# Layer 1's pooling mixer and cross-attention in one plan, its queries by seven products; readers of a PSUM bank due by the bank's next user

## The chip, the cores and the metric

The kernel runs on one core of a Trainium2 chip. Five engines work beside each other, each through its own instructions in order: PE (TensorE, matrix products), DVE (VectorE), ACT (ScalarE), POOL (GpSimd) and SP (here the queue that issues all the DMAs). They wait for each other by semaphores. The metric is the device time of one execution in microseconds. All data are float32; a product of two float32 matrices is made from three matmuls on a "high" and a "low" part of each operand (`mm3`: high·high, high·low, low·high), in a reduced format called fp32r.

## The reference, cut to what matters

```python
def reference(x, mem, ...):
    for i in range(2):
        if i == 0:                                   # layer 0
            x = x + axial_gqa_attention(rmsnorm(x, attn_norm[0]), ...)
        else:                                        # layer 1
            x = x + multiscale_pool_mixer(rmsnorm(x, pool_norm[0]), pool_w[0], pool_scale[0])
        x = x + memory_cross_attention(rmsnorm(x, xattn_norm[i]), rmsnorm(mem, mem_norm[i]),
                                       xattn_w_q[i], xattn_w_kv[i], xattn_w_o[i])
        x = x + conv_gated_ffn(rmsnorm(x, ffn_norm[i]), ...)
    return rmsnorm(x, final_norm)

def multiscale_pool_mixer(h, w_grp, scale):          # h is (1024, 1024)
    # per group of 256 channels: centred mean over 2/4/8/16 tokens, minus the token itself,
    # then a 256x256 matrix per group, and a scale per channel
    mixed = (s_hi - s_lo) / count - hg
    return einsum('bsgc,gcd->bsgd', mixed, w_grp) * scale

def memory_cross_attention(h, mem_n, w_q, w_kv, w_o):  # 4 heads of 256, 256 memory tokens
    q = h @ w_q * 256 ** -0.5                        # (1024, 1024) @ (1024, 1024)
    k, v = split(mem_n @ w_kv)
    return softmax(q @ k.T) @ v @ w_o
```

## The kernel before, in words

The 1024 tokens are eight row tiles `X[0]` to `X[7]` of 128 rows by 1024 columns, which stay in SBUF. There are 20 operand tiles `R` (each in two halves), and six scratch tiles `scr` of 128 x 1024. PSUM is two buffers `pA` of 1024 columns and four banks `pB` of 512.

Most of the program is made by a planner (class `Plan`). A function hands it operations, each with the engine, an assumed duration, what it reads and writes, which buffers it takes, and sometimes a due time `late`. The operations on PE stay in the order in which they were handed over. Those of the other engines are sorted by a due time, counted back from the PE operation that needs them, and the planner then writes every engine's instructions in that order. The attention of layer 0 and, before the change, the pooling mixer and cross-attention of layer 1 are written out by hand instead.

The large products of layer 0's cross-attention (its queries) and of both gated MLPs go by class `Seven`: Strassen's scheme with seven products instead of eight. Eight block sums of the right operand (`B11`, `B21`, `B22`, `T1` to `T4`) are made from the transposed row tiles, in pairs of an even and an odd tile, and block sums of the weights (`A11`, `A12`, `S1` to `S4`, `A22`) on DVE. A transposed row tile goes through `turn` (PE, eight transpositions), `take1` and `take2` (ACT and DVE).

The stage that the change touches lies between the last products of layer 0's MLP and the output matrix of layer 1's cross-attention. Before, it runs so:

- `pool_weights` fetches the mixer's weights and scales them, behind the plan of layer 0's MLP.
- `pool_mixer` goes through 16 steps. In each, the entries of `POOL_ORDER` are called in turn, each with a lag in steps. "rest" (`down`, L1747 on) makes two products of six matmuls for one row tile and adds them to `X` (DVE, L1757); "fetch" (L1800) copies a piece of 128 rows, shifted against the tiles so that each gives 112 rows of means, from `X` to a scratch tile by DMA; "scale" normalises it (square on ACT L651, 1/rms on POOL L643 and L645, scaling on ACT L1812); "mix" (L1819) multiplies it with a band matrix on PE; its result is split into high and low on ACT (L590) and DVE (L591); "out" makes the group matrices' products (24 matmuls of 256 columns) and adds them to `X` (DVE, L1836); "norm" (L656) and "turn" (L664) normalise and transpose a row tile for the queries; "go" makes the first queries.
- `cross_queries` makes the rest of the queries by plain products of 24 matmuls of 512 columns, 16 of them, and in between halves of the sums of layer 1's MLP weights (`down_sums`, L1418). `cross` then makes the memory's keys and values, scores, softmax (ACT L1352, POOL L1356) and values. `X` stays where it is during all this.

```python
POOL_ORDER = ((0, "rest"), (2, "stage"), (3, "split"), (5, "norm"), (1, "fetch"), (10, "go"), (6, "split2"),
              (4, "stage2"), (12, "go2"), (4, "out"), (1, "scale"), (2, "mix"), (5, "turn"))
```

Of the kernel before, what the change touches and what calls it, by code (L numbers as in the profile page):

```python
# [16 lines left out]
P = 128  # L17
# [13 lines left out]
XH = 4  # L31
# [7 lines left out]
POOL_ORDER = ((0, "rest"), (2, "stage"), (3, "split"), (5, "norm"), (1, "fetch"), (10, "go"), (6, "split2"),  # L39
              (4, "stage2"), (12, "go2"), (4, "out"), (1, "scale"), (2, "mix"), (5, "turn"))  # L40
# [43 lines left out]
class Slots:  # L84
# [43 lines left out]

    def put_half(self, *hs):
        self.clock += 1  # L130
        for h in hs:
            self.freed[h] = self.clock if self.now is None else self.until

    def v(self, i, a):
        return self.tiles[i].rearrange("p (a b) -> p a b", a=a)

# [4 lines left out]
class Plan:  # L141
# [18 lines left out]
    def add(self, kind, n, emit, reads=(), writes=(), take=(), uses=(), gives=None, late=None):  # L160


        engine, least, each, lag = self.KINDS[kind]
# [23 lines left out]

    def run(self):
        pools = self.pools
        for op in reversed(self.ops):  # L190
            for o in op["after"]:
                o["due"] = min(o["due"], op["due"] - o["lag"])
# [60 lines left out]
        self.slots.timed(False)  # L253


class Seven:
# [6 lines left out]
    def __init__(self, kn, w, columns, X, Xd, gain):  # L263
        self.kn, self.nc, self.R = kn, kn.nc, kn.R
        self.w, self.columns, self.X, self.Xd, self.gain = w, columns, X, Xd, gain
        self.H, self.raws, self.place, self.ops, self.bank, self.ps, self.r = {}, {}, {}, {}, {}, {}, {}

# [136 lines left out]
    def begin(self, gemm, add, free, between):  # L404

        late, split = self.late, self.split
# [26 lines left out]

    def plan_rest(self, plan):

        X = lambda t, h: (f"X{t}", h)
        nc, lo, hi = self.nc, self.LO, self.HI

        def keep(name, t, src, *keys, uses=()):
            parts = lambda: self.parts(name, t)  # L440
            shaped = lambda: src().rearrange("p (a b) -> p a b", a=4)
            plan.add("copy", 512, lambda: self.kn.high(list(parts())[0], shaped()), keys, [("H", name, t)], uses=uses)
            plan.add("add", 512, lambda: self.kn.low(*parts(), shaped()), [*keys, ("H", name, t)], [("H", name, t)], uses=uses)

        def sub(out, p, q, reads, writes, uses=(), late=None):
            plan.add("add", 512, lambda: self.sub(nc.vector, out(), p(), q()), reads, writes, uses=uses, late=late)

        t = NT - 1
        x, y = self.X[t - 1], self.X[t]
        ps = lambda g: lambda: self.ps[t][g]  # L450
        at = lambda ap, h: lambda: ap[:, h]
# [1494 lines left out]
```

## Time and profile before

| | |
|---|---|
| median of 3 runs | 2574.74 us (2573.03 to 2577.07) |
| the profiled execution | 2578.49 us, its span 2576.7 us |
| PE busy | 2516.0 us, 98% of the span |
| DVE, ACT, POOL busy | 1950.9, 1329.6, 380.6 us |
| the stage that the change touches | 1547.36 to 1832.76 us of the span |

In the views, a line such as L1757 is a line of the kernel before; `out<-in` are the tiles' names without their numbers; `PEld` is PE loading weights, which overlaps `PE`. A matmul's recorded end is modelled, so a busy PE can still be waiting a little. The rows of windows give busy time of each engine, with the number of instructions in brackets, then the granted clock of PE as a share of full speed (`PEclk`), the share of DMA time and GB/s. A row of the time line ends with the idle time of the engine before it and what ended it.

### The profile page before, as it was taken

How to read it: one execution, taken by the hardware profiler on the slowest of the kernel's cores; microseconds unless marked ns; L12 is line 12 of the kernel's file. 1: busy time of each engine (PE TensorE's matmuls, PEld its weight loads, DVE VectorE, ACT ScalarE, POOL GpSimd, SP SyncE). 2: the span in 40 equal slices, each digit the busy share in tenths (PEclk: the TensorE clock that was granted, in tenths of full speed). 3: DMA queues.
4: the chain of work that ended last, by engine and by line, in shares of the span. 5: the costliest groups of instructions: out<-in, count | busy, mean ns of one | idle time of the engine just before them, and what ended most of it. 6: DMA issues, size and time to landing. Idle time of an engine off the chain costs nothing. (4 is left out here: it accounts for less than half of the span.)

```text
span 2576.7 us, 36870 instructions
## 1 busy us (share of the span) xinstructions
PE 2516.0 (98%) x13529; PEld 2149.3 (83%) x13529; DVE 1950.9 (76%) x2857; ACT 1329.6 (52%) x2244; POOL 380.6 (15%) x523
## 2 busy tenths in 40 slices
PE   8999999999999999999999998999999999999998
PEld 7988888888898888888877887889788888887886
DVE  5778999974886389888878756654559988888775
ACT  4447888863555255555455425424436554555441
POOL 3664554530002000000000001102010000000001
PEclk9999999999999999999999999999999999999999
DMA  4200000042485134243358633581223333337751
GB/s 157 83 9 1 1 2 1 2 152 66 160 310 206 42 90 123 82 123 103 94 175 275 209 125 91 179 311 50 88 78 94 113 91 113 113 98 267 235 184 65
DMA packets 289801, 306.79 MB, mean 119 GB/s; under 512 B 12245, under 2 KB 230717, under 8 KB 289621
## 3 DMA queue, kind: packets, MB, share of 16 engines
q1 hardware_dynamic: 289621, 304.45, 36.5%
q8 instruction: 106, 1.74, 0.3%
q14 instruction: 74, 0.61, 0.1%
HBM read 223.04 MB, written 76.55 MB: 116 GB/s over the span
## 5 line engine op out<-in xcount | busy, mean ns | idle before, releaser
L670 PE MATMUL pB<-R,R 128*128 128x512 f32 (+1 forms) x2708 | 1013.5, 375 | 4.5 <-ACT R L590 1.9
L671 PE MATMUL pB<-R,R 128*128 128x512 f32 (+1 forms) x2708 | 1007.0, 372 | 1.8 <-DVE R L591 1.7
L672 PE MATMUL pB<-R,R 128*128 128x512 f32 (+1 forms) x2700 | 1003.3, 372 | 2.5 <-DVE R L585 2.5
L670 PEld LDWEIGHTS pB<-R,R 128*128 128x128 f32 x2708 | 510.2, 189 | 98.5 <-ACT R L590 3.0
L671 PEld LDWEIGHTS pB<-R,R 128*128 128x128 f32 x2708 | 510.4, 188 | 90.3 <-DVE R L591 3.5
L672 PEld LDWEIGHTS pB<-R,R 128*128 128x128 f32 x2700 | 508.4, 188 | 91.6 <-DVE R L585 3.3
L582 ACT ACTIVATE R<-scr 128x512 fp32r<-128x512 f32 (+2 forms) x283 | 205.8, 760 | 207.3 <-PE pB L671 58.0
L643 POOL TENSOR_SCALAR ms<-ss 128x1 f32<-128x1 f32 (+2 forms) x102 | 27.3, 267 | 1698.8 <-ACT scr L651 675.0
L585 DVE TENSOR_TENSOR R<-X,R 128x512 fp32r<-128x512 f32 x339 | 228.9, 686 | 65.1 <-ACT R L582 65.1
L582 ACT ACTIVATE R<-X 128x512 fp32r<-128x512 f32 x339 | 210.9, 630 | 100.5 <-PE pB L671 64.5
L585 DVE TENSOR_TENSOR R<-scr,R 128x512 fp32r<-128x512 f32 (+2 forms) x283 | 232.4, 851 | 13.9 <-ACT R L582 13.8
L394 ACT COPY scr<-pB 128x512 f32<-128x512 f32 x144 | 84.4, 587 | 187.9 <-PE pB L672 182.5
L664 PE MATMUL pB<-ident,scr 128*128 128x128 f32 x1232 | 163.8, 276 | 10.3 <-DVE scr L656 7.9
L664 PEld LDWEIGHTS pB<-ident,scr 128*128 128x128 f32 x1232 | 140.7, 143 | 35.6 <-POOL scr L729 14.9
L729 POOL TENSOR_SCALAR scr<-scr,inv 128x1024 f32<-128x1024 f32 x128 | 144.6, 1129 | 166.6 <-DVE inv L728 161.7
L670 PE MATMUL pA<-R,R 128*128 128x512 f32 (+1 forms) x460 | 161.6, 351 | 6.7 <-ACT R L582 2.3
L1673 DVE TENSOR_TENSOR X<-pB,X 128x512 f32<-128x512 f32 x144 | 99.3, 691 | 89.3 <-PE pB L672 86.8
L591 DVE TENSOR_TENSOR PT<-pB,PT 128x512 fp32r<-128x512 f32 x256 | 163.9, 681 | 3.0 <-ACT PT L590 2.0
L726 ACT ACTIVATE scr<-pA,nm 128x1024 f32<-128x1024 f32 x128 | 143.0, 1117 | 44.6 <-DVE nm L723 42.5
L672 PE MATMUL pA<-R,R 128*128 128x512 f32 (+1 forms) x460 | 160.8, 350 | 1.7 <-DVE R L591 0.8
L671 PE MATMUL pA<-R,R 128*128 128x512 f32 (+1 forms) x460 | 160.1, 348 | 0.5 <-DVE R L585 0.5
L723 DVE TENSOR_REDUCE nm<-pA 128x1 f32<-128x1024 f32 x128 | 156.1, 1219 | 0.9 <-PE pA L719 0.4
(157 smaller groups left out, 3596.7 us busy)
## 6 DMA issues: line engine op xcount, KB each, us to landing
X<-in_ffn_w_up SPq DMA_DIRECT2D x82, 512.0 KB
scr<-in_ffn_w_down SPq DMA_DIRECT2D x54, 512.0 KB
Gs<-X SPq DMA_DIRECT2D x100, 256.0 KB
scr<-Gs SPq DMA_DIRECT2D x56, 384.0 KB
scr<-Wt SPq DMA_DIRECT2D x40, 512.0 KB
scr<-in_xattn_w_kv SPq DMA_DIRECT2D x32, 512.0 KB
Wt<-scr SPq DMA_DIRECT2D x60, 256.0 KB
scr<-Gs SPq DMA_DIRECT2D x28, 512.0 KB
```

Of the source, the lines that this page charges most:

```text
L394: self.nc.scalar.copy(out, p)
L582: self.nc.scalar.activation(hi, src, AF.Copy)
L585: self.nc.vector.tensor_tensor(out=lo, in0=src, in1=hi.bitcast(F32), op=OP.subtract)
L591: nc.vector.tensor_tensor(out=lo, in0=src, in1=hi.bitcast(F32), op=OP.subtract)
L664: self.nc.tensor.transpose(p[:, k, :], src[:, b * P:(b + 1) * P], self.ident)
L670: mm(out, ah, bh, start=start, stop=False)
L671: mm(out, ah, bl, start=False, stop=False)
L672: mm(out, al, bh, start=False, stop=stop)
L723: nc.vector.tensor_reduce(nm, s, axis=AX.X, op=OP.max, negate=True)
L726: nc.scalar.activation(pr, s, AF.Exp, bias=nm, accum_out=rs)
L729: nc.gpsimd.tensor_scalar(pr, pr, ri, 1.0, op0=OP.mult, op1=OP.mult)
L1673: nc.vector.tensor_tensor(out=x, in0=banks[b], in1=x, op=OP.add)
```

## The change

`pool_mixer`, `cross_queries`, `cross` and `memory` of layer 1 go; the planned function that made layer 0's cross-attention (`cross_planned`, now `cross`) makes both layers'. For layer 1 it first hands the planner the mixer (`MIXER`: D for the last products of layer 0's MLP, M for mix, O for out, T for a row tile's transpositions and its block sums, in the order even tiles first), then the queries as seven products for each of four pairs of column blocks. A piece's scaling goes from ACT to POOL. `X` is saved to DRAM (`Xq1`) after the mixer, since its tiles are then used as buffers, and loaded again at the end. The mixer's weights are prepared inside the plan of layer 0's MLP, at the start of its third round. In all plans, `releases` gives those operations that read a PSUM bank a due time before the PE operation that takes the bank next; a set of operand tiles is taken when its first part is written, and the transposed probabilities may lie in single halves (`get_pair`).

```diff
-POOL_ORDER = (...)
+MIXER = ("D0", "D1", "D2", "D3", "D4", "D5", "D6", "M0", "D7", "M1", "O0", "M2", "M3", "O2", "T0", "M4", "M5", "M6", "O4",
+         "T2", "M7", "O1", "O6", "T4", "M8", "M9", "O3", "O5", "T6", "T1", "O7")
...
+    def releases(self):
+        at = {id(op): i for i, op in enumerate(self.ops)}
+        ends = {k: max(at[id(o)] for o in ops) for k, ops in self.users.items()}
+        soft, out = {}, {"A": [], "B": []}
+        for i, op in enumerate(self.ops):
+            for pool, held in out.items():
+                new = [k for p, k in op["take"] if p == pool]
+                if new and op["engine"] == "PE":
+                    n = len(held) + len(new) - len(self.room[pool])
+                    for k in [k for k in held if ends[k] < i][:max(n, 0)]:
+                        held.remove(k)
+                        soft.setdefault(i, []).extend(o for o in self.users[k] if o["engine"] != "PE")
+                    held += new
+        return soft
...
     def run(self):
         pools = self.pools
-        for op in reversed(self.ops):
-            for o in op["after"]:
+        soft = self.releases()
+        for i, op in reversed(list(enumerate(self.ops))):
+            for o in op["after"] + soft.get(i, []):
                 o["due"] = min(o["due"], op["due"] - o["lag"])
...
+    def plan_early(self, plan):
+        self.raws[0], self.place[0] = [None] * 3, [f"raw0{j}" for j in range(3)]
+        self.plan_load(plan, 0, 0, 1, new={0: (0, 2), 1: (1,)})
+        self.plan_left(plan, 0, *self.EVERY, late=14.0)
...
+            plan = Plan(R, over, {"scr": 2 if steps else 6, "A": 2, "B": 4, "half": len(R.freed)})
+            if mixer:
+                mixer(plan, U, X)
+                order[:4] = [(2, 0), 3, (1, 0), 5, (2, 1), None]
...
-            nc.scalar.activation(y, y, AF.Copy, scale=rs)
+            def scale():
+                nc.gpsimd.tensor_scalar(Y[j][:m], Y[j][:m], ps.pop(r), 1.0, op0=OP.mult, op1=OP.mult)
+            plan.add("load", 1, fetch, [k for t in covers(j) for k in both(t)], [y], [("scr", y)])
+            plan.add("square", 1024, square, [y], [r], [("half", junk)], [y, junk])
+            plan.add("scale", 2.5, scale, [y, r], [y], uses=[y])
...
+            def save():
+                nc.sync.dma_start(out=U.Xd[t * P:(t + 1) * P, :], in_=X[t])
...
+        U.plan_early(plan)
+        for what, n in MIXER:
+            {"D": plan_rows, "M": plan_mix, "O": plan_out, "T": partial(U.plan_turned, plan)}[what](int(n))
...
+            for n, _ in enumerate(phase):
+                if n == 55 and extra:
+                    extra(plan)                      # pool_weights, layer 0 only
...
-            ops = self.cross(i, *self.cross_queries(i, hT, *ready["q"])) if i else self.cross_planned(i, lhs, X, free, ws)
+        lhs, *ops = self.cross(0, X, steps)
+        gemm, add, over = self.ffn(0, lhs, X, *ops, lambda plan: ready.extend([self.pool_weights(plan)]))
+        lhs, *ops = self.cross(1, X, None, partial(self.pool_mixer, gemm, add, ready[0]), over)
+        gemm, add, _ = self.ffn(1, lhs, X, *ops)
```

Three places show what moved. The first is DVE at the start of the stage, from the first rows that add the MLP's last products to `X`. Before:

```order
L1778 SCALAR_TENSOR_TENSOR scr<-scr,pgain 128x256
L1757 TENSOR_TENSOR X_7410<-pB,X_7410 128x512 x2
L591 TENSOR_TENSOR R_72<-scr,R_84 128x1024
L1757 TENSOR_TENSOR X_7412<-pB,X_7412 128x512 x2
L1757 TENSOR_TENSOR X_7405<-pB,X_7405 128x512 x2
L591 TENSOR_TENSOR R_67<-pA,R_69 128x8x112
```

And now (L1658 adds to `X`, L389 makes a sum of weight blocks, L663 the low part of one):

```order
L1658 TENSOR_TENSOR X_7410<-pB,X_7410 128x512 x2
L389 TENSOR_TENSOR scr<-scr 128x512
L1658 TENSOR_TENSOR X_7412<-pB,X_7412 128x512
L663 TENSOR_TENSOR R_81<-scr,R_81 128x512
L1658 TENSOR_TENSOR X_7412<-pB,X_7412 128x512
L389 TENSOR_TENSOR scr<-scr 128x512 x2
L1658 TENSOR_TENSOR X_7405<-pB,X_7405 128x512
L663 TENSOR_TENSOR R_70<-scr,R_70 128x512
L663 TENSOR_TENSOR R_68<-scr,R_68 128x512
L663 TENSOR_TENSOR R_74<-scr,R_74 128x512
L663 TENSOR_TENSOR R_67<-scr,R_67 128x512 x2
L1658 TENSOR_TENSOR X_7406<-pB,X_7406 128x512
```

The mixer's weights (L1778, L591 from `scr`) have left this place; the sums and low parts of the first weight blocks of the queries (11 operations of 128 x 512) stand between the adds instead. Some rows that only repeat are left out.

The second is the DMA queue (SP). Before, the weights of the queries come behind the first piece:

```order
L1800 DMA scr<-X_7410 120x1024
L1802 DMA scr<-X_7410 8x1024
L614 DMA scr<-in_xattn_w_q 128x4x256
L1800 DMA scr<-X_7410 24x1024
L1800 DMA scr<-X_7412 104x1024
L1800 DMA scr<-X_7412 40x1024
```

Now they come ahead of it, and `X` is saved between the pieces (L1822):

```order
L370 DMA scr<-in_xattn_w_q 128x8x128 x2
L1747 DMA scr<-X_7410 120x1024
L1749 DMA scr<-X_7410 8x1024
L1747 DMA scr<-X_7410 24x1024
L1747 DMA scr<-X_7412 104x1024
L1747 DMA scr<-X_7412 40x1024
L1747 DMA scr<-X_7407 40x1024
L1822 DMA Xq_14807<-X_7410 128x1024
L1747 DMA scr<-X_7407 104x1024
```

Three of the six scratch tiles hold the queries' first weight blocks and their sums at that time, one the gain and one the band; the pieces take what is left, and get more as the weight blocks are split.

The third is DVE where the last odd row tiles are transposed (L337 takes a transposed tile, L314 normalises, L663 makes low parts; `R_86` is the operand `T1` of the third product, with a row for each odd tile, and `R_70` the low part of `S1` for the second pair of column blocks). Before, the stage had at this place, for each tile:

```order
L656 SCALAR_TENSOR_TENSOR scr<-X_7407,rs,scr 128x1024
L594 SCALAR_TENSOR_TENSOR R_74<-pB,R_74 128x512
L1836 TENSOR_TENSOR X_7409<-pA,X_7409 128x1024
L591 TENSOR_TENSOR R_68<-pA,R_70 128x8x112
L591 TENSOR_TENSOR R_79<-pB,R_76 128x4x128
L591 TENSOR_TENSOR R_71<-pB,R_80 128x4x128
```

Now the end of that stretch is:

```order
L314 SCALAR_TENSOR_TENSOR X_7411<-X_7411,rs,scr 128x1024
L337 TENSOR_TENSOR X_7408<-pB,X_7408 128x512
L663 TENSOR_TENSOR R_79<-X_7412,R_76 128x4x128
L337 TENSOR_TENSOR X_7409<-pB,X_7409 128x512
L663 TENSOR_TENSOR R_86<-X_7410,R_84 128x4x128
L663 TENSOR_TENSOR R_86<-X_7405,R_84 128x4x128
L663 TENSOR_TENSOR R_86<-X_7408,R_84 128x4x128
L663 TENSOR_TENSOR R_86<-X_7409,R_84 128x4x128
L337 TENSOR_TENSOR X_7411<-pB,X_7411 128x512
L663 TENSOR_TENSOR R_85<-pB,R_71 128x4x128
L663 TENSOR_TENSOR R_70<-X_7406,R_70 128x512
```

What was one normalisation and two splits for a tile is now a normalisation, up to three subtractions and the splits of two to four operands.

More of the change, by code (lines that the diff above doesn't have):

```diff
@@ L253, in run @@
         self.slots.timed(False)
+        self.over = {e: max(0.0, t - self.free["PE"]) for e, t in self.free.items()}
 class Seven:
@@ L432, in begin, with plan_turned @@
                 self.take2(u)
-    def plan_rest(self, plan):
+    def plan_turned(self, plan, t):
+        nc, lo, hi = self.nc, self.LO, self.HI
         X = lambda t, h: (f"X{t}", h)
[L437 to L449, printed above, removed]
+        x, y = self.X[t - t % 2], self.X[t]
```

622 lines of the change are left out of this document (268 added, 354 removed).

## The prediction

> **What bounds the kernel now.** I read the page first, then the windows of the stage and of stages like it, then PE's waits in the stage, then the time line where it starts.
>
> ```profile
> PE 2516.0 (98%) x13529; PEld 2149.3 (83%) x13529; DVE 1950.9 (76%) x2857; ACT 1329.6 (52%) x2244; POOL 380.6 (15%) x523
> PE 33%; DMA 2%; DVE 1%; ACT 1%; issue 1%; POOL 1%; SPq 0%; DVEq 0%; POOLq 0%; ACTq 0%
> ```
>
> PE is busy for 98% of the span, and in the chain that ended last it holds more than all others together. So time goes if PE gets fewer products or waits less. The windows tell where it waits (busy PE, PEld, DVE, ACT, POOL, then clock, DMA share, GB/s):
>
> ```profile
> 1547.36:1832.76 285.40, 268.84 (x1650) 239.29 (x1650) 172.31 (x233) 133.78 (x248) 36.48 (x72) 0.98 0.47 158
> 600.00:830.00 230.00, 227.41 (x1326) 198.19 (x1325) 170.60 (x242) 115.42 (x229) 28.83 (x48) 1.00 0.60 204
> 830.00:1335.00 505.00, 504.91 (x2260) 417.89 (x2259) 396.08 (x529) 247.42 (x372) 8.53 (x18) 1.00 0.33 100
> 1675.00:1700.00 25.00, 25.00 (x112) 20.71 (x111) 14.86 (x21) 5.12 (x7) 0.00 (x0) 1.00 1.01 373
> 75.00:100.00 25.00, 25.00 (x217) 25.00 (x216) 21.43 (x51) 14.26 (x26) 15.96 (x21) 1.00 0.27 85
> 1755.00:1790.00 35.00, 31.95 (x244) 31.13 (x245) 16.70 (x22) 17.72 (x48) 10.38 (x16) 0.95 0.19 61
> ```
>
> The first row is the stage: 16.6 us idle on PE, clock 0.98. The second is layer 0's cross-attention, planned and by seven products: 2.6 us idle in 230, clock 1.00. The third is layer 0's MLP, with 0.1 idle in 505. Undisturbed, a matmul of 512 columns takes 25.00 / 111 = 0.225 us (fourth row, plain queries) and one of 256 takes 25.00 / 216 = 0.116 us (fifth). The stage has 576 of the first, 768 of the second, 144 transpositions and 160 small products of pieces at about 0.12 each: 129.6 + 89.1 + 17 + 19 = 255 us. It takes 285.4, so it loses **about 30 us**: 16.6 idle, about 6 half clock (0.02 of 285), the rest refilling behind each wait. Its named waits:
>
> ```profile
> PE pA L1819 <- ACT scr L1812: 6.2, 1, 6.2
> PE pA L670 <- ACT scr L1352: 2.2, 2, 1.7
> PE pA L670 <- ACT R L590: 2.1, 2, 1.5
> PE pB L670 <- ACT R L590: 1.9, 4, 0.7
> PE pB L671 <- DVE R L591: 1.5, 2, 0.9
> PE pB L664 <- DVE R L591: 1.1, 1, 1.1
> PE pA L672 <- DVE R L591: 0.8, 2, 0.5
> ```
>
> They and two of 0.2 sum to 16.2. The longest is the first piece, which the time line shows:
>
> ```profile
> 1553.90 0.97 SPq L1800 DMA_DIRECT2D scr<-X  x1
> 1559.23 1.06 ACT L651 ACTIVATE R<-scr 128x1024 fp32r<-128x1024 f32 x1 [5.41 <-DMA scr<-X]
> 1560.46 0.19 POOL L643 TENSOR_SCALAR ms<-ss 128x1 f32<-128x1 f32 x1 [627.55 <-ACT R L651]
> 1560.74 0.55 POOL L645 TENSOR_TENSOR rs<-ms,mh 128x1 f32<-128x1 f32 x1
> 1561.32 1.15 ACT L1812 ACTIVATE scr<-scr,rs 128x1024 f32<-128x1024 f32 x1 [0.94 <-POOL rs L645]
> 1562.52 3.75 PE L1819 MATMUL pA<-scr 128*128 128x112 f32 x16 [6.16 <-ACT scr L1812]
> ```
>
> Fetch 5.3 us, square to root 2.1, scaling 1.2: 8.6 us from the issue, and PE has nothing else for 6.2 of them. Its products then run at half clock (3.75 us for 16).
>
> **The change part by part.** *Products:* 16 plain products of 24 matmuls become 4 x 7 of 12, so 336 for 384: 48 x 0.225 = **-10.8 us**. All other matmuls stay. The stage's floor goes from 255 to 244.
>
> *DVE:* it must make the block sums of queries and weights, and rebuild the results. Counted in its order: 80 more operations of 512 columns, 8 fewer of 1024, 8 more of 256. The groups of the stage price them:
>
> ```profile
> L591 DVE TENSOR_TENSOR R<-scr,R 128x1024 fp32r<-128x1024 f32 x34 | 41.6, 1236 | 16.9 <-ACT R L590 14.8 <-PE pB L671 1.9
> L591 DVE TENSOR_TENSOR R<-pB,R 128x512 fp32r<-128x512 f32 x52 | 33.4, 684 | 3.9 <-ACT R L590 3.8
> L656 DVE SCALAR_TENSOR_TENSOR scr<-X,rs,scr 128x1024 f32<-128x1024 f32 x8 | 10.3, 1283 | 5.2 <-POOL rs L645 5.2
> L591 DVE TENSOR_TENSOR R<-pB,R 128x256 fp32r<-128x256 f32 x16 | 6.7, 423 | 19.7 <-ACT R L590 19.7
> ```
>
> 80 x 0.684 - 8 x 1.236 + 8 x 0.423 = +48 us, so about 221 of some 262: 84% busy, beside 74% in layer 0's planned stage and 78% in the MLP. On average it fits under PE; in places it cannot, and these I walk below.
>
> *Pieces:* ten scalings go from ACT to POOL. Whole tiles were scaled there in layer 0's attention:
>
> ```profile
> L729 POOL TENSOR_SCALAR scr<-scr,inv 128x1024 f32<-128x1024 f32 x128 | 144.6, 1129 | 166.6 <-DVE inv L728 161.7
> ```
>
> 1.13 for 1.15 us: nothing, alone. Behind a scaling on POOL stand the roots (0.19 and 0.55) of the next piece and of the row tiles, which normalise on DVE: one of them may come 1.13 later, which is in the two waits of T below. ACT loses ten scalings, gains a dozen half copies, and at 134 of 285 us stays far from a bound. Beside DVE it may cost. The time line has one pair:
>
> ```profile
> 627.57 1.29 POOL L298 TENSOR_TENSOR X<-X,X 128x512 f32<-128x512 f32 x1 [6.07 <-DVE X L298]
> 628.00 1.41 DVE L591 TENSOR_TENSOR R<-X,R 128x512 fp32r<-128x512 f32 x1
> ```
>
> There DVE takes 1.41 for 0.684, the time until POOL is done and its own. Ten scalings cost DVE between 0 and 10 x 1.13 = 11.3 us. I take half, 5.6, of which only what falls into a DVE-bound stretch reaches PE: about 1, inside the terms below. [...]
>
> *Saving `X`:* eight 512 KB writes behind the adds and eight loads at the end. Layer 0 does the same with its loads and loses 0.1 in the row of 830 to 1335; I take 0. On SP the saves stand between the pieces' fetches, and the next piece could issue up to one issue (0.97) later each: up to 1 us in M, in the range.
>
> *Weights of the mixer:* moved into the MLP's third round, where PE never waits (0.1 idle): 0. *Banks' readers due by the next user:* this re-sorts ACT and DVE in every plan. What it could win is the idle of the planned stages other than this one, 2.6 here and in
>
> ```profile
> 1335.00:1420.00 85.00, 81.42 (x352) 65.27 (x351) 71.62 (x99) 46.32 (x67) 0.00 (x0) 1.00 0.77 257
> 2332.00:2420.00 88.00, 84.64 (x366) 67.91 (x366) 74.24 (x103) 48.36 (x69) 0.00 (x0) 1.00 0.76 257
> ```
>
> 3.6 and 3.4, at most 9.6 in all; but the last two lie where DMA is at 0.77 and DVE at 84%, and sorting fetches nothing sooner. An early bank read also pushes some operand back. Between -9.6 and +9.6, I take 0, the nearest to the 0.1 of the MLP.
>
> *New waits in the stage*, walked from the first add product (t = 0) with the orders of the engines and the rows' durations. A half-row product of D is 6 x 0.225 = 1.36, M 1.9, O 24 x 0.116 = 2.8, T 0.9, one of the seven 12 x 0.225 = 2.7.
> - D: DVE's second add ends at 3.5; the eighth add stands 17 operations later (the weight sums between), 3.5 + 17 x 0.69 = 15.2. The twelfth half-row needs that bank at 11 x 1.36 = 15.0: **0.4 with handover**. Piece 0 is issued at 3.5 and ready 8.7 later at 12.2; M0 comes at 14 x 1.36 = 19: its 6.2 wait is **gone**. What is late next is piece 1: its scratch tile comes free when the low part of a weight block ends at about 12.7, plus a queue place, ready at about 23; M1 is due at 19 + 1.9 + 2.7 + 0.4 = 24. It just fits.
> - M1 to O0: the small split is 0.28 on ACT and 0.29 on DVE: **0.6**. M3 to O2: ACT has two squares (1.06 each) ahead of the copy, one of a piece that lands only about 31.5: **2.2**.
> - T6 and T3 wait for a normalisation (1.28) behind the add: **0.6 each**.
> - From O7 to the third product of the second pair: DVE has 20 operations of 0.69 and 3 of 1.28 = 17.6, PE 14.9 of work: **3.3** with handovers; the next product, 6 x 0.69 against 2.7 and a little slack: **1.0**.
> - Half clock after such waits: **2**. The 1755 row has 0.95 with a longest wait of 1.7 (softmax), so short waits do cost clock. [...]
> - The rest as in layer 0's stage: 2.6 idle, 4 with refill.
>
> Sum 0.4 + 0.6 + 2.2 + 1.2 + 4.3 + 2 + 4 = 14.7. Not all of a loss is visible as a wait: in the stage before, 30 were lost for 16.6 idle and 6 of half clock, 30 / 22.6 = 1.33. I scale the waits that I walked, but not the last term, which has its refill: 10.7 x 1.33 + 4 = 18. The stage becomes 244 + 18 = **262**, 23.4 less than 285.4. The profiled execution took 2578.49, its span 2576.7; it becomes 2555. It lies 0.15% above the median of the runs, 2574.74, so the median becomes **2551**.
>
> **The rivals.**
> - *DVE bounds the whole turning stretch.* From T1 to the last product of the second pair DVE has 52 operations, some 37.6 us, against PE's 39; there is no reserve, so POOL's lock (5.6) and a handover of 0.5 at each of five products go straight to PE. For it: 84% busy, with 78% only in the MLP. Against: layer 0 passes the same turning at 74% with 2.6 idle. Some 8 us more: 2559.
> - *As smooth as layer 0.* The stage loses 6 as 600 to 830 does (2.6 idle and refill): 244 + 6 = 250, 35 less: 2540. For it, the same planner; against, the mixer's chains have no counterpart there.
> - *The old losses return.* New waits take the place of those removed, 30 in all: only the 10.8 of products remain: 2564. [...]
> - *Slower: the pieces go through one scratch tile.* At the start three of six hold weight blocks and two the gain and band. If no second tile comes free, each piece waits until the one before is multiplied: 8.6 + 1.9 + handover = 10.8, ten times 108 us from t = 3.5, against PE's own work up to the last O of 16 x 1.36 + 10 x 1.9 + 8 x 2.8 + 5 x 0.9 = 68: +44, with 23.4 gone: 2574.7 + 20 = 2595. It decides from the point where fewer than two tiles turn over. Against: the weight blocks are split by about 16 us, and three more tiles are then free.
> - *The change does not do what it says*: the queries' matmuls would stay 384. The order on PE has 336, so no chance of its own.
>
> **How the numbers follow.** Forecast 0.50 (own range 2546 to 2556), DVE-bound 0.20, as smooth as layer 0 0.12, old losses 0.12, slower 0.06. The range 2538 to 2567 takes the first four with their bounds, leaving out the slower case and the tails. A measurement of this kernel tells about 0.2% (5 us) from no change. Slower by more: 0.06. Within: 0.05, the tail of the old losses with the bank order at its worst. Faster: 0.89.
>
> **What would show it.** In the profile after: 336 matmuls of 512 for the queries, a stage of about 262 us with 8 to 13 us idle; no wait of PE for the first piece; one of 1 to 3 us at O2 and several on DVE's low parts (R<-X) in the products (5, 0) and (5, 1) ahead of them; DVE near 221 us; 600 to 830 and 830 to 1335 unchanged within 2 us, the rows at 1335 and 2332 within 3. It is wrong if PE waits for pieces in M1 to M9 for over 5 us (scratch tiles), if a wait on the saved `X` or the first operands of the MLP appears behind the stage, or if the other plans change by more than 5 us in sum.

## The result, and the profile after

The changed kernel takes 2550.24 us (median of 4 runs, 2548.18 to 2550.72), the kernel before 2574.97 us (4 runs beside it): a ratio of 0.9902, 95% interval 0.9885 to 0.9919, or 24.7 us less. The forecast was 2551.

The windows of the changed kernel (busy PE, PEld, DVE, ACT, POOL with instructions, then clock, DMA share and GB/s) show the stage, its first 23 us (the MLP's last products), the stretch in which the last row tiles are turned, and two stretches of other plans:

```profile
1547.37:1805.49 258.12, 250.77 (x1601) 224.27 (x1600) 204.85 (x298) 145.51 (x284) 46.60 (x82) 1.00 0.59 202
1547.37:1570.00 22.63, 22.63 (x108) 18.77 (x107) 17.15 (x26) 7.18 (x13) 3.94 (x8) 1.00 0.35 94
1612.00:1640.00 28.00, 24.81 (x145) 20.70 (x144) 26.49 (x41) 19.57 (x35) 3.42 (x6) 1.00 0.20 75
830.00:1335.00 505.00, 504.49 (x2256) 416.84 (x2255) 400.39 (x534) 249.51 (x376) 8.53 (x18) 1.00 0.34 103
1335.00:1420.00 85.00, 81.27 (x351) 65.17 (x350) 71.14 (x99) 46.03 (x67) 0.00 (x0) 1.00 0.77 254
```

The stage begins at 1547.37, as it did before (1547.36), and ends with the same matmul at 1805.49 where that was 1832.76. It is 258.1 us for 285.4, **27.3 less**; what follows it takes 2548.9 - 1805.49 = 743.4 for 743.9. The whole difference lies in the stage. (The two profiled executions differ by 27.8 and the medians by 24.7, since the profiled execution before was 3.5 us above its median and the one after 0.5.) PE's idle in the stage falls from 16.6 to 7.4 us, and the clock column says 1.00 for 0.98: PE was at half clock for 13.7 us of the stage before, for none of it now. Fewer products (10.8), less idle (9.2) and no half clock (about 6) are 26 of the 27.3.

The waits of PE in the stage, in us: total, times, longest:

```profile
PE pB L741 <- DVE X L337: 1.4, 1, 1.4
PE pB L741 <- ACT X L483: 1.0, 1, 1.0
PE pB L741 <- ACT R L660: 0.9, 2, 0.6
PE pB L741 <- DVE R L663: 0.9, 3, 0.4
PE pB L741 <- DVE scr L435: 0.8, 1, 0.8
PE pA L1771 <- PE pA L1771: 0.6, 1, 0.6
PE pB L743 <- DVE R L663: 0.5, 1, 0.5
PE pB L319 <- DVE X L314: 0.4, 1, 0.4
PE pB L1088 <- DVE scr L435: 0.3, 1, 0.3
```

The first piece's 6.2 is not among them; the longest is 1.4, at 1632.83 on the time line, where the product (1,1) comes behind the turning of row tile 7. ((n, f) is product n of the seven for pair f of column blocks. Counted on the time line, the matmul that waits there is the first of (1,1), and the 0.4 at 1638.96 is at the first of (5,1); some of the expectations below call the two (1,0) and (5,0).) The page's first part, for the totals:

```profile
PE 2497.3 (98%) x13481; PEld 2135.8 (84%) x13481; DVE 1992.3 (78%) x2937; ACT 1344.8 (53%) x2286; POOL 386.7 (15%) x533
```

PE has 48 matmuls fewer, DVE 80 operations and 41 us more. In the stage DVE has 204.9 us, not the 221 of the forecast, since not all of the new work lies in it: of the 80 operations, 65 do. The scaling and splitting of the mixer's weights, ten operations, went from the stage to the MLP, where DVE has 86.7 us for 81.4 between 1420 and the stage, and behind the stage it has 567.5 for 562.7. The forecast's sum took neither off. The rest of the 16, some 6 us, was not followed line by line.

### The profile page after: what moved, and what is told of

Read it like the earlier page. It is cut to its first block, busy times and chain, and to the rows that moved or that the text cites. A ratio compares the mean times of both kernels' runs of the same rounds, so it can differ in the third digit from the quotient of the medians.

```text
span 2548.9 us, 37005 instructions
## 1 busy us (share of the span) xinstructions
PE 2497.3 (98%) x13481; PEld 2135.8 (84%) x13481; DVE 1992.3 (78%) x2937; ACT 1344.8 (53%) x2286; POOL 386.7 (15%) x533
## 4 chain that ended last, share of the span: by engine, by line
PE 80%; DVE 9%; issue 3%; ACT 3%; POOL 2%; DMA 2%; SPq 0%; DVEq 0%; ACTq 0%; POOLq 0%
PE pB L741 21%; PE pB L743 21%; PE pB L742 21%; PE pA L743 3%; PE pA L741 3%; PE pA L742 3%; DVE nm L780 2%; PE pB L735 2%; PE pA L776 2%; PE pB L1007 1%; POOL qn L852 1%; DVE R L663 1%; DVE PT L669 1%; PE pB L1008 1%; ACT scr L783 1%
## 5 line engine op out<-in xcount | busy, mean ns | idle before, releaser
L741 PEld LDWEIGHTS pB<-R,R 128*128 128x128 f32 x2750 | 518.1, 188 | 102.2 <-DVE R L663 3.4
L743 PEld LDWEIGHTS pB<-R,R 128*128 128x128 f32 x2730 | 514.3, 188 | 92.1 <-DVE R L663 5.3
L742 PEld LDWEIGHTS pB<-R,R 128*128 128x128 f32 x2750 | 518.3, 188 | 86.4 <-DVE R L669 0.7
L660 ACT ACTIVATE R<-scr 128x512 fp32r<-128x512 f32 (+2 forms) x318 | 237.0, 780 | 238.8 <-DMA scr<-Gs 59.6
L663 DVE TENSOR_TENSOR R<-X,R 128x512 fp32r<-128x512 f32 x374 | 252.1, 685 | 65.7 <-ACT R L660 64.9
L660 ACT ACTIVATE R<-X 128x512 fp32r<-128x512 f32 x374 | 231.7, 630 | 133.8 <-PE pB L742 65.5
L663 DVE TENSOR_TENSOR R<-scr,R 128x512 fp32r<-128x512 f32 (+2 forms) x318 | 271.0, 882 | 23.8 <-ACT R L660 23.8
L433 ACT COPY scr<-pB 128x512 f32<-128x512 f32 x156 | 91.2, 586 | 196.9 <-PE pB L743 191.0
L735 PE MATMUL pB<-ident,scr 128*128 128x128 f32 x1088 | 144.6, 276 | 9.1 <-DVE scr L727 7.9
L741 PE MATMUL pA<-R,R 128*128 128x512 f32 (+1 forms) x416 | 149.5, 359 | 2.5 <-ACT R L660 2.5
L735 PEld LDWEIGHTS pB<-ident,scr 128*128 128x128 f32 x1088 | 124.2, 142 | 32.7 <-POOL scr L786 14.9
L743 PE MATMUL pA<-R,R 128*128 128x512 f32 (+1 forms) x416 | 148.9, 358 | 0.5 <-DVE R L663 0.5
L742 PE MATMUL pA<-R,R 128*128 128x512 f32 (+1 forms) x416 | 148.6, 357 | 0.5 <-DVE R L663 0.5
```

What stands on the lines that cost most here:

```text
L433: self.nc.scalar.copy(out, p)
L660: self.nc.scalar.activation(hi, src, AF.Copy)
L663: self.nc.vector.tensor_tensor(out=lo, in0=src, in1=hi.bitcast(F32), op=OP.subtract)
L735: self.nc.tensor.transpose(p[:, k, :], src[:, b * P:(b + 1) * P], self.ident)
L741: mm(out, ah, bh, start=start, stop=False)
L742: mm(out, ah, bl, start=False, stop=False)
```

## The experiments

All times below are medians. They come from three chips, on each of which the kernel before took 2578.4 to 2578.9 us, so they are set side by side; with four runs each, a difference of 2 us or less between two of them is not told from none, and one of 3 barely. Stage times come from the traces, from the first of the MLP's last products to the matmul that ends the stage. Line numbers shift by a few from kernel to kernel.

**The changed kernel again** (base for the rest).

> The changed kernel again, as the base for the kernels beside it: its stage 258.1 us in the trace within 1 us, its time 24.7 us under the kernel before within 4.

2552.05 us against 2578.38, 26.3 less, ratio 0.9898 (0.9883 to 0.9913); stage 258.5.

**48 matmuls put back** (is PE what sets the end?).

```diff
+        for _ in range(12 if n == 5 and not self.began else 0):
+            self.nc.tensor.matmul(u[bank], ah[:, 0], bh[:, 0], start=True, stop=True)
         for k in range(4):
             self.kn.mm3(...)
```

> The changed kernel with 48 matmuls of 512 columns put back: ahead of each of the four products (5, f) of the queries, twelve matmuls that the product then overwrites, so PE has as many of them as before the change. Theory (PE sets the end in the whole stage, the waits left are short): +48 x 0.225 = +10.8 us, 2561, within 1.5. Rival (DVE sets the end in the stretch in which (5,0) and (5,1) stand): the first 24 fall into PE's waits and cost nothing, +5.4 at most, 2555.6 or less.

2565.92 us (2559.93 to 2566.63), 13.9 over the base, which is more than the 10.8 and outside the 1.5 allowed; one of the four runs is only 7.9 over. The stage is 269.7, 11.2 longer by the trace, of which up to 1.7 is a window at half clock (below), so 9.5 without it; another such window lies outside the stage. The 48 matmuls are thus paid for in full or nearly so, and the rival's 5.4 at most is out by both measures. Where the rest of the 13.9 comes from is not shown.

**Eight operations more on DVE, and eight fewer, where the last row tiles are turned** (does DVE set the pace there?).

```diff
+        def low():
+            for _ in range(2 if name in ("T1", "B22") and not self.began else 1):
+                self.kn.low(*parts(), shaped())
```

> The changed kernel with eight more operations of 512 columns on DVE (0.69 each by their rows) between T1 and the product (5,1): the low parts of T1 and B22 of the four odd tiles are made twice. Theory (PE sets the end, DVE follows close behind): 8 x 0.69 = 5.5 less a small reserve, +2 to +4 us. Rival (DVE sets the end there): the whole, +4.8 to +5.5. If DVE were off the path by more than it: 0.

```diff
+        if name in ("T1", "B22") and not self.began:
+            plan.add("copy", 512, lambda: self.kn.high(list(parts())[1], shaped()), ...)
+            return
         plan.add("add", 512, lambda: self.kn.low(*parts(), shaped()), ...)
```

> The changed kernel with the low parts of T1 and B22 of the four odd tiles written by ACT as plain copies (0.6 each, ACT is busy for half of the stretch) and not by DVE: the values are not the reference's, the amount of work is the same but for 8 operations (5.5 us) taken off DVE between T1 and (5,1). Theory A (DVE's amount of work sets the pace there): the four waits of that stretch (0.4 before T6, 1.0 before O7, 1.4 before (1,0), 0.4 before (5,0), with their refilling 3.9) go down by 2.5 to 4 us. Theory B (they are latencies: an operation that cannot begin earlier, whatever DVE has to do): 0 to -1 us.

The second edit leaves the low parts out: ACT writes plain copies in their place, so the products are not the reference's, and eight operations go from DVE to ACT.

With eight more: 2555.33 us, 3.3 more than the base; stage 263.9, 5.4 more, with one window at half clock in it, behind the longest wait. The time line of PE shows where (start, us, and in brackets the wait before):

```profile
1632.67 0.77 PE L745 MATMUL pB<-R,R 128*128 128x512 f32 x1 [3.60 <-DVE X L337]
1638.49 0.50 PE L746 MATMUL pB<-R,R 128*128 128x512 f32 x1 [1.06 <-DVE R L667]
1642.43 0.47 PE L745 MATMUL pB<-R,R 128*128 128x512 f32 x1 [1.16 <-DVE R L667]
```

The wait at (1,1) grows from 1.4 to 3.6, and those at (5,0) and (5,1), which the forecast had at 3.3 and 1.0, appear with about 1.1 each. With eight fewer: 2551.91 us, stage 258.9 with one window at half clock, so 0.4 more or, without that window, some 1.3 less. Its waits:

```profile
PE pB L745 <- ACT R L664: 2.4, 3, 1.4
PE pB L745 <- ACT X L483: 1.0, 1, 1.0
PE pB L745 <- DVE scr L435: 0.8, 1, 0.8
```

The wait at (1,1) is still 1.4, and that at O7 is still 1.0. The row puts the wait at (1,1) down to ACT, but on the time line it is the same wait as in the changed kernel: PE starts 0.15 us behind a subtraction on DVE that reads a PSUM bank (L337, `X<-pB`; it ends at 1632.69 and PE starts at 1632.83 there, 1634.23 and 1634.37 here), while ACT's operation ends after PE has started. And in the stretch ahead DVE now waits for the copies that were given to ACT:

```profile
1627.38 0.69 DVE L337 TENSOR_TENSOR X<-pB,X 128x512 f32<-128x512 f32 x1 [1.15 <-ACT R L664]
1628.74 0.69 DVE L337 TENSOR_TENSOR X<-pB,X 128x512 f32<-128x512 f32 x1 [0.67 <-ACT R L664]
```

That is 1.8 us, so this run does not tell the amount of DVE's work from a latency behind the other engine. What is shown: DVE has next to no reserve there (more work is paid for by 3.3 to 5.4 of 5.5 us; the forecast's theory of a close follower holds by the times, and by the trace once the half clock is taken off, while the trace's 5.4 taken whole would be the rival's). In the changed kernel DVE runs without idle from 1620.43 to 1636.29, and the wait at (1,1) ends with one of its operations. What less work on DVE alone would bring stays open.

**The pieces' scaling back on ACT.**

```diff
-                nc.gpsimd.tensor_scalar(Y[j][:m], Y[j][:m], ps.pop(r), 1.0, op0=OP.mult, op1=OP.mult)
+                nc.scalar.activation(Y[j][:m], Y[j][:m], AF.Copy, scale=ps.pop(r))
...
-            plan.add("scale", 2.5, scale, ...)
+            plan.add("centre", 1024, scale, ...)
```

> The changed kernel with the pieces' scaling on ACT, as it was before the change (ten operations of 1.15 us there, ten of 1.13 fewer on POOL). Theory (POOL's scalings cost DVE little, since DVE is not the bound while they run): 0, within 1.5 us. Rival (each scaling holds DVE up): 4 to 8 us faster. Third: ACT holds up the copies that O0 and O2 wait for: 2 to 5 us slower.

2553.86 us, 1.8 over the base, which these runs can't tell from none; stage 261.8, 3.3 more, with one window at half clock. The rival's gain of 4 to 8 us is not there. The waits for ACT's split at O0 and O2 grew from 0.9 to 2.0 us and the one at (1,1) from 1.4 to 2.5, so the third theory has its mechanism in the trace, if not its size in the times. What the scaling on POOL costs DVE is in DVE's groups, first of the changed kernel, then with the scaling on ACT:

```profile
L663 DVE TENSOR_TENSOR R<-scr,R 128x512 fp32r<-128x512 f32 x9 | 7.2, 834 | 0.0
L314 DVE SCALAR_TENSOR_TENSOR X<-X,rs,scr 128x1024 f32<-128x1024 f32 x8 | 10.7, 1334 | 0.0
```

```profile
L663 DVE TENSOR_TENSOR R<-scr,R 128x512 fp32r<-128x512 f32 x9 | 5.9, 685 | 0.2 <-ACT R L660 0.2
L314 DVE SCALAR_TENSOR_TENSOR X<-X,rs,scr 128x1024 f32<-128x1024 f32 x8 | 10.2, 1276 | 0.0
```

1.3 + 0.5 = 1.8 us in these two groups, 1.2 in DVE's whole time in the stage (204.9 for 203.6), on an engine that has room while the pieces are scaled.

**The due times of the PSUM banks' readers alone, in the kernel before.**

```diff
+    def releases(self): ...                          # as in the change
...
+        soft = self.releases()
-        for op in reversed(self.ops):
-            for o in op["after"]:
+        for i, op in reversed(list(enumerate(self.ops))):
+            for o in op["after"] + soft.get(i, []):
```

> The kernel before with only the due times for the readers of PSUM banks. They change no engine's order in the two plans of the MLPs, and 79 rows of DVE and 74 of ACT in layer 0's cross-attention. Theory: 0, within 1.5 us (2574.97). Rival: it takes the waits of that stage, 2.6 us idle and as much of refilling: -2.6 to -5. Third: operands come later instead, up to +5.

2575.91 us against 2578.67, ratio 0.9988 (0.9979 to 0.9998): 2.8 less, at the edge of the interval. In the stretch that they can change, PE's waits in the kernel before and then with them are

```profile
PE pB L1214 <- DVE R L585: 0.9, 2, 0.5
PE pB L670 <- DVE scr L396: 0.8, 1, 0.8
PE pB L280 <- DVE X L275: 0.7, 1, 0.7
```

```profile
PE pB L297 <- DVE X L292: 1.0, 1, 1.0
PE pB L687 <- DVE scr L413: 0.8, 1, 0.8
PE pB L687 <- DVE R L602: 0.5, 2, 0.3
PE pB L1111 <- DVE scr L413: 0.3, 1, 0.3
```

2.4 and 2.6 us: other waits, nearly the same sum. No gain is shown in them. Of the 2.8 by which the two profiled spans differ as well, 1.6 lies in the stage of the mixer (283.8 for 285.4), which these due times don't touch and which has 10.2 us at half clock for 13.7, one window less; the rest stays without a place. The changed kernel without these due times was not run, so what they bring there is not shown.

**One scratch tile for all pieces** (the slower rival's condition, forced).

```diff
+        plan.room["one"] = [0.0]
...
-            plan.add("load", 1, fetch, ..., [y], [("scr", y)])
+            plan.add("load", 1, fetch, ..., [y], [("scr", y), ("one", ("one", j))])
...
-            plan.add("product", 8.25 * n / PIECE, mix, [("piece", j)], [b], [("A", b)], [("piece", j), "band"])
+            plan.add("product", 8.25 * n / PIECE, mix, [("piece", j)], [b], [("A", b)], [("piece", j), ("one", j), "band"])
```

> The changed kernel with its pieces through one scratch tile, each fetched only when the one before has been multiplied. By the walk of the prediction's slower rival, a piece takes 10.8 us from issue to the end of its products, ten of them 108 from t = 3.5 against 68: +44 us in the stage, 302. Theory B (most of a piece's chain lies behind the products of O and T): under +15.

2592.74 us, 40.7 over the base and slower than the kernel before; stage 298.7, 40.2 more. The waits and the stage's row:

```profile
PE pA L1772 <- POOL scr L1758: 27.4, 7, 7.5
```

```profile
1547.75:1846.41 298.66, 263.85 (x1601) 235.83 (x1600) 205.78 (x298) 145.23 (x284) 45.67 (x82) 0.93 0.52 175
```

PE waits for seven pieces, 27.4 us, and its clock over the stage is 0.93; the rest of the 40 is half clock (41 us of the stage, in part the waits themselves) and refilling behind these waits. The rival's mechanism and price were right (+44 by the walk); only its condition doesn't hold, for in the changed kernel enough scratch tiles turn over.

**The first piece's wait in the kernel before, filled with small matmuls** (what did the half clock behind it cost?).

```diff
+            for _ in range(0 if j else 48):
+                nc.tensor.matmul(p[:, 0, :n], self.ident, band[:, 0, :n], start=True, stop=True)
```

> The kernel before with 48 small matmuls (128 x 112, 0.12 us each = 5.6 us) ahead of the first piece's products, into the columns that these then overwrite. They come when the piece is ready, so the wait of 6.2 stays. Theory A (PE at half clock for 6.8 us after that wait, whatever it does): the 48 run at half clock too, and the rest at full: about +5.6 +1 us. Theory B (half clock lasts for so many matmuls): the first 16 products stay slow, +9 to +11.

2579.66 us, ratio 1.0003 (0.9993 to 1.0013). The experiment was not what its expectations say: the small matmuls need nothing of the piece, so they ran in the wait, and each is two instructions (x96 for 48). On PE, in the kernel before, and then here:

```profile
1562.52 3.75 PE L1819 MATMUL pA<-scr 128*128 128x112 f32 x16 [6.16 <-ACT scr L1812]
1569.72 1.93 PE L1819 MATMUL pA<-scr 128*128 128x112 f32 x16
```

```profile
1557.39 10.87 PE L1819 MATMUL pA<-scr,ident 128*128 128x112 f32 x96
1568.10 1.95 PE L1821 MATMUL pA<-scr 128*128 128x112 f32 x16
1572.67 1.93 PE L1821 MATMUL pA<-scr 128*128 128x112 f32 x16
```

It still answers the question. Kept busy, PE does the first piece's products in 1.95 us where it took 3.75 after the wait, and from the first to the second piece's products 4.57 for 7.20: the half clock (0.50 from 1561.1 to 1567.9 in the kernel before, so 1.4 us of it lie still in the wait) cost 2.6 us. Since the filling overran the wait by over 4 us, nothing is won. The wait for the first piece was thus worth 6.2 + 2.6 = 8.8 us, about half of the 16.5 by which the stage's losses fell.

**Other orders of the mixer.** The first puts O7 ahead of T6 and T1; the second also each O of the first half one M later; the third has the outputs in the order of the row tiles. In all three, the product (2,0) is no longer held back until the sums of row tile 6 are written (the planner's list of what a product reads names the odd tiles only, which is enough in the change's order), so it multiplies what stood there; the amount of work is the same, but a wait that (2,0) would have is left out.

```diff
-MIXER = (... "M8", "M9", "O3", "O5", "T6", "T1", "O7")
+MIXER = (... "M8", "M9", "O3", "O5", "O7", "T6", "T1")
```

> The changed kernel with O7 ahead of T6 and T1 in the mixer's order (and nothing else by hand). Theory (the waits at T6, for a normalisation, and at O7, for a PSUM bank that T6 still holds, come from this order): the 0.4 and 1.0 us of wait with their refilling, 1.7, go, and the stage is 256.4 to 257.4 by the trace. Rival (the wait moves on to the next row tile's turn, whose operands are as late): 258.1 to 258.6, no change.

```diff
-MIXER = (... "M0", "D7", "M1", "O0", "M2", "M3", "O2", "T0", "M4", "M5", "M6", "O4", "T2", "M7", ... "T6", "T1", "O7")
+MIXER = (... "M0", "D7", "M1", "M2", "O0", "M3", "M4", "O2", "T0", "M5", "M6", "O4", "M7", "T2", ... "O7", "T6", "T1")
```

> As the one beside it, and each O of the first half one M later (M1, M2, O0, M3, M4, O2, ...), so that the small splits get 1.9 us of cover. Theory: O0's 0.9 and O2's 0.6 us of wait go too, 3 to 3.7 in all: stage about 255. Rival (the next piece isn't ready one M sooner, since it comes through a scratch tile that is freed late): a wait for a piece instead, 2 us or more, stage 257 to 262.

```diff
+MIXER = (... "M0", "D7", "M1", "O0", "M2", "O1", "M3", "O2", "T0", "M4", "O3", "M5", "O4", "T2", "M6", "O5", "M7", "O6", "T4", "M8", "M9", "O7", "T6", "T1")
```

> The changed kernel with the mixer's outputs in the order of the row tiles (O0, O1, O2, ... O7), the even tiles' turns as soon as their output is there: no even tiles first. Theory (even first spreads the turns' work on DVE under the odd outputs): T4 and T6 and their block sums come late and close together, and DVE's 0.60 us a step holds up the first products: +2 to +5 us in the stage. Rival (the order of O does not matter while the pieces set the pace): within 1 us.

O7 first: 2555.06 us, stage 262.7 with two windows at half clock; the waits at T6 and O7 are gone, and the one at (1,1) is 3.6 for 1.4. The rival was right: the wait moved on, though how much of the 3.6 would stand at (2,0) had that product waited is not shown. O later and O7 first: 2552.52 us, stage 264.0 with three windows at half clock (some 5 us); O0's and O2's waits for ACT are gone, the same 3.6 stands at (1,1), and 2.0 us appear for row tiles' normalisations. Outputs in a row: 2563.41 us, 11.4 over the base; stage 270.5. Its waits say why, and it is not the expected reason:

```profile
PE pB L740 <- ACT R L659: 6.1, 8, 1.1
PE pB L742 <- DVE R L662: 3.6, 7, 0.6
PE pB L740 <- DVE X L336: 2.6, 1, 2.6
```

Each O then stands right behind the M that makes its last columns, and waits for the split of that M on ACT and DVE, eight times: 9.7 us of waits. The order of the change puts another M or O between. Most of what "even tiles first" brings in these runs is cover for that split, not room for DVE's block sums.

**A version from these readings.** One M between each M and its O in the first half, T6 ahead of O5, but T1 and O7 last as in the change; and the products' reads name all row tiles.

```diff
-MIXER = (... "M1", "O0", "M2", "M3", "O2", "T0", "M4", "M5", "M6", "O4", "T2", "M7", "O1", "O6", "T4", "M8", "M9", "O3", "O5", "T6", "T1", "O7")
+MIXER = (... "M1", "M2", "O0", "M3", "M4", "O2", "T0", "M5", "M6", "O4", "T2", "M7", "O1", "O6", "T4", "M8", "M9", "O3", "T6", "O5", "T1", "O7")
...
-        plan.add("product", 12, emit, [op] + [("H", right, t) for t in (1, 3, 5, 7)], ...)
+        plan.add("product", 12, emit, [op] + [("H", right, t) for t in range(NT)], ...)
```

> The changed kernel with each O of the first half one M later, T6 ahead of O5, and T1 and O7 last as in the change (M1 M2 O0 M3 M4 O2 T0 M5 M6 O4 T2 M7 O1 O6 T4 M8 M9 O3 T6 O5 T1 O7); the first two products also wait for the even row tiles' sums by name, so that no order can run past them. Theory (the waits at O0, O2 and the piece between are the splits' latency, those at T6 and O7 a bank held by T6): 0.9 + 0.6 + 0.6 us of wait and up to 1.4 more go with their refilling, stage 254.5 to 256.5 by the trace, the time 2 to 4 us under the change. Rival (as when O7 went first, they move on to the product (1,0) and to a row tile's normalisation): 257.5 to 259.5, no change.

2546.85 us (2545.31 to 2549.34), ratio to the kernel before 0.9876 (0.9860 to 0.9893): 5.2 us under the base, all four runs below the base's lowest. Its waits and its stage:

```profile
PE pB L740 <- DVE X L336: 1.3, 1, 1.3
PE pB L740 <- DVE R L662: 0.9, 3, 0.4
PE pB L742 <- DVE R L662: 0.9, 2, 0.5
PE pB L740 <- DVE scr L434: 0.8, 1, 0.8
```

```profile
1548.36:1802.60 254.24, 249.74 (x1601) 224.21 (x1600) 203.47 (x298) 145.13 (x284) 47.23 (x82) 1.00 0.61 205
```

The waits for ACT at O0, O2 and O7, the one before M and the one for T6 are gone, and only one of 0.4 for a split on DVE has come: 254.2 us, 4 less, and 5.2 in the times, both a little beyond the theory's upper end. The 1.3 at (1,1) stays. By its times it beats both kernels, though it ran on another chip than the base and the two intervals against the kernel before still overlap a little; the stage's 4 us in the trace are the firmer reading.

## Why the prediction was right, point by point

**Products, -10.8.** Putting 48 back costs 9.5 to 11.2 in the trace and 13.9 in the times. Right, and the rival by which half of it would vanish in waits is out. The floor itself is a little low: the row of 75 to 100 from which 0.116 was read holds some 40 transpositions among its 217 matmuls. From start to start a matmul of 256 columns takes 0.120 us in the stage, one of 512 0.227, a piece's 0.112 and a transposition 0.109, so the floor of the changed stage is 245.6 rather than 244.2.

**The first piece's wait.** Right: none is left, and the walk's times were close. It is fetched, squared and scaled 12.6 us after the stage's start (12.2 by the walk), the second at 23.7 (23), just ahead of M1 at 23.8 (24). On the time line of the changed kernel:

```profile
1551.05 0.97 SPq L1747 DMA_DIRECT2D scr<-X  x1
1558.35 1.66 POOL L1757 TENSOR_SCALAR scr<-scr,rs 128x1024 f32<-128x1024 f32 x1
1569.94 1.13 POOL L1757 TENSOR_SCALAR scr<-scr,rs 128x1024 f32<-128x1024 f32 x1
1571.19 1.98 PE L1771 MATMUL pA<-scr 128*128 128x112 f32 x16
```

What was called "late next" is late by nothing: the second piece is ready 0.1 us before it is wanted. There is no reserve there.

**The new waits, sized 18 together, measured 13.9** (258.1 less the floor of 244.2 that the forecast used). By terms:

| term | forecast, before scaling | measured |
|---|---|---|
| banks in D | 0.4 | 0 (PE 22.63 of 22.63 busy) |
| O0, O2 | 0.6 and 2.2 | 0.4 + 0.5 and 0.6 |
| T6, T3 | 0.6 each | 0.4; at T3 none, but 1.0 at O7 and 1.4 at (1,1) |
| (5,0), (5,1) | 3.3 and 1.0 | none and 0.4 |
| half clock | 2 | 0 in this stage |

The term that was mis-sized most is the stretch of 23 operations on DVE before (5,0), and one step that failed is the duration used for each. The rows' mean is 0.69 us, but in these rows DVE's operations overlap a little where they follow each other. A row of the kernel before showed it already, and one of the changed kernel in that very stretch does:

```profile
1554.99 2.48 DVE L1757 TENSOR_TENSOR X<-pB,X 128x512 f32<-128x512 f32 x4
```

```profile
1633.20 3.09 DVE L663 TENSOR_TENSOR R<-X,R 128x512 fp32r<-128x512 f32 x5
```

Four in 2.48 and five in 3.09, the last with its whole 0.69: 0.60 us from start to start. The 23 operations took 15.9 us together (1620.43 to 1636.29) for the walk's 17.6, against PE's 14.9. The other step is a wait that the walk did not have: PE waits 1.4 at (1,1), inside the same stretch, so that (5,0) finds its low parts in time. It and the 1.0 at O7 are waits for a PSUM bank, which the walk followed in D but not in the turning. The stretch loses 1.8 us where the walk had 4.3.

The walk's terms were 10.7 us; the waits at their places and the 0.6 before one M sum to 5.3, half. Times 1.33 that is 7.1, so the rest of the stage loses 6.8, for which the forecast had 4 (5.4 by the floor of 245.6). Two errors of opposite sign, and the larger one was in the walk.

**DVE as the bound** (chance 0.20): out at its price, since the waits in the turning stretch are 1.8 us where the rival added 8. (POOL's lock, which it counts with 5.6, is the 1.41 for 0.684 us of the forecast's time line; the scaling cost DVE 1.2 us over the whole stage.) As what sets the pace inside that stretch DVE is not out: it is 26.5 of 28 us busy between 1612 and 1640, and the next 5.5 us cost 3.3 to 5.4. **ACT**, which was to lose ten scalings and gain a dozen half copies, has 145.5 us in the stage for 133.8: more operations came to it than were counted. At 56% it is no bound, but three of the waits (O0, O2, O7) are for it. **As smooth as layer 0** (6 lost): not reached by the change, but the reordered version, with 10 by the same sum, comes nearer to it than the forecast did. **Old losses return:** no. **Scratch tiles:** the mechanism costs what was said, where it is forced.

**Edits costed at nothing.** The scaling on POOL is that, or a little better than nothing (with it on ACT the waits for the splits grow). The mixer's weights and the saving of `X`: the stage starts at the same time as before, what follows is 0.5 us shorter, and no wait names them. The banks' due times: the times say -2.8 and the waits say nothing; the forecast's 0 within 9.6 holds, and 1.6 of the 2.8 is one window of half clock in a stage that they don't touch.

**Signs.** Of the signs that the prediction named, the missing wait for the first piece and the unchanged other stages came. PE's idle is 7.4 us for 8 to 13, the wait at O2 0.6 for 1 to 3, DVE's low parts hold up (5,1) by 0.4 and (5,0) by nothing, and DVE has 205 us for 221.

**Why it came out at 2550 all the same.** The stage gained 27.3 where 23.4 was forecast, 3.9 more. The forecast also took the 3.5 us by which the profiled execution before lay above its median to be there in the changed kernel's too; it has 0.5. The two errors cancel to 0.8. One reason is that the stage varies from run to run: in the kernel before with the banks' due times alone, where it is untouched, it took

```profile
1547.06:1830.85 283.79, 266.42 (x1649) 237.38 (x1649) 172.54 (x233) 133.64 (x248) 37.89 (x72) 0.98 0.48 159
```

that is 283.8 for 285.4, one window of half clock less; and the changed kernel's stage happened to have none (see the last section). So part of the agreement is luck.

## What to carry to other kernels

Price a chain of operations on one engine by the step from start to start in the time line, not by the mean duration of a group: here 0.60 for 0.69 us. In a stretch in which PE is 89% and DVE 95% busy, extra work on either was paid for. The waits behind a split (O0, O2) went by putting one independent piece of work between producer and user (M2 between M1 and O0); when an order only shifts, a wait can move on to the next bank. Taking work off an engine by giving it to another tests both at once. Walk PSUM banks through every place where they are taken in pairs, and cost a wait with the slow clock behind it: the 6.2 us here were 8.8.

## What the runs showed of the hardware that was not expected

PE runs at half clock for 3.4 us at places with no wait near. In the kernel with 48 matmuls put back, and in the one with eight operations off DVE, no wait stands within 15 us ahead of these rows:

```profile
1610.50:1613.50 3.00, 3.00 (x16) 3.00 (x16) 0.69 (x1) 0.47 (x1) 0.00 (x0) 0.50 0.00 0
```

```profile
1609.00:1612.00 3.00, 3.00 (x15) 3.00 (x15) 0.69 (x1) 0.00 (x0) 0.00 (x0) 0.50 0.00 0
```

PE has work throughout, and the clock is 0.50; each such window costs about 1.7 us. The changed kernel, with the same instructions at that place, has none in either of its two profiled executions. The traces tell the place. Where one has several half-clock stretches, their starts lie whole multiples of 3.413 us apart (in the changed kernel 29.16, 189.59 and 2541.37 us: 47 and 689 times), which gives a grid for the whole trace. Just ahead of both rows stand the 16 products of the last piece, of only 16 columns, which take 1.9 us. In five traces these lie within one step of the grid (the two above, O7 first, O later with O7 first, and the kernel before, where they run from 1629.97 to 1631.93 in the step from 1629.37 to 1632.78), and in all five the next step is at half clock. In eight, with both of the changed kernel and the reordered version among them, none is, and where their clock gives the grid a boundary falls into the 1.9 us (in the changed kernel at 1606.12, with the products from 1606.04 to 1608.00). (With one scratch tile PE is at half clock there already.) So whether the window comes depends in these traces on where the grid falls, which is luck, and 1.7 us of the difference between the two stages is that, by this pattern. Why these products bring it was not tested.

Behind waits half clock came as well: 6.8 us of it with the 6.2 us wait before, 3.4 us behind a wait of 1.7 there (it ends at 1755.38, the clock falls at 1755.7) and behind one of 1.7 with O later (at 1597.3), and with one scratch tile, at 27.4 us of waits for pieces, the clock of the stage is 0.93. In the changed kernel's stage the longest wait is 1.4 us and none came, so the prediction's term of 2 us was 0 there. The term was an average over something that comes or doesn't.

POOL and DVE hold each other up both ways, but rarely: POOL's scaling of a whole tile took 1.13 us alone and 1.66 beside DVE (the first piece), 1.91 once more and 1.11 to 1.13 in the other eight; one DVE split beside the first piece took 1.53 for 0.68, and nine of DVE's splits 834 ns for 685 in the mean; the two groups that differ sum to 1.8 us for ten scalings, of a possible 11.3. In the kernel before, the six operations of DVE (`R<-X,R`) that start beside POOL's six `X<-X,X` take 1.40 to 1.42 us for 0.684, as the prediction's pair does. How often the two meet is the kernel's own order, and can only be read from a trace.
